# The four HGRN value tiles as one token-major group at the head of the layer

## The chip, the cores and the metric

The program runs on one core of one Trainium2 chip. The metric is the device time of one execution in microseconds. The engines are TensorE (PE; PEld is its weight load), VectorE (DVE), ScalarE (ACT), GpSimd (POOL) and SyncE (SP), which issues most of the DMAs.

## What is computed

Two layers over 640 tokens (128 of context, 512 latent; five token tiles of 128), model width 2048 (16 k-tiles), all in float32. Cut to what matters here, a layer is

```
h = x * (1 + scale) + shift                  # adaLN, from the conditioning vectors
z = h @ w_in_l                               # 2048 -> 6656 columns
aq, ak, av, ag, hq, hi, hff, hfb, hgate, ca, cb, cgate = split(z)
v = hi                                       # HGRN values, 4 heads of 128
hg_out = rms_norm(hgrn2(silu(hq), v, gates(hff)) + hgrn2 backward (gates(hfb)))
att = windowed attention with a sink;  cv = conv module
mix = concat(att * silu(ag), hg_out * silu(hgate), cv * silu(cgate))
x = LayerNorm(ALPHA * x + gate * (mix @ w_out_l))
```

Only `hi` (512 columns of `w_in`) and the order of the other tiles are concerned. A float32 product is made of three float32r matmuls: every operand is split into a high and a low part (`HH`, `HL` for the activations, two `wh` slots for a weight chunk), and high x high, high x low and low x high are accumulated.

## The kernel before

The activations lie as `HH`/`HL`: 128 model channels in the partitions, by token tile and k-tile. The projection is made in 52 tiles of 128 output columns (`NTILES`), feature-major: `mm` (L1162) takes a 128x128 weight block as the stationary operand and streams the 640 tokens past it, as 256 tokens (L1173) and 384 (L1175) into two PSUM banks. A tile is 16 k-tiles x 3 products x 2 matmuls. Two such PSUM tiles (`zt`) alternate; four single banks (`mb`) serve everything else.

The order of the tiles is: for each HGRN head j the tiles `hff`, `hfb`, `hi`, `hq`; then the four `hgate`; then attention's `ak`, `av`, `aq`; the conv tiles; the remaining gates. After each tile, a generator that evacuates it is put in the list `active`; behind `hq` also `hg_main` (L505), the HGRN computation of that head. The order of the instructions on each engine is written out by `pump` (L260): after every half of a weight chunk (eight times per tile) it advances up to three of the active generators by one step, and at a rate given by `RATE` the modulation of later stages, which `ada_dve` computes on VectorE (L362). If a PSUM tile or a scratch slot (`S`, nine of them) isn't free when the program is written, `pump_until` advances the generators until it is. `hg_main` takes 27 steps to the head's output; the heads hold a lock, one after the other, and there are two sets of HGRN buffers.

HGRN needs its values token-major (tokens in the partitions, as `lhsT` of L693 and right operand of L664), so `e_hi` (L482) copies the tile to scratch on ScalarE and `to_tokens` (L471) transposes it with five matmuls against the identity (L474, L478) and copies the result on ScalarE (L475, L479) into the head's buffer `v`.

Weights come in chunks of 128 x 512 float32 (256 KB), four to a tile. `w_load1` (L1117) loads one over SP into one of eight `raw` slots, `w_split` (L1129) splits it into two of 16 `wh` slots. The split has three forms: ScalarE copies the high part and VectorE subtracts (L286, L287); GpSimd does both (L284, L287); or ScalarE copies the high part and its negative (L290, L291) and a DMA from GpSimd's queue adds the weight from HBM onto it (L292, `split_add`). In the run of a layer the last form is used, one tile ahead (`ahead`, L1238).

**Start of layer 0.** `ada_pe` computes scale and shift on TensorE from 64 weight tiles of 512 KB (L317, ten `x` buffers), for eight pairs of k-tiles one after the other. `after0` (L1190) builds those two k-tiles of `HH`/`HL` and then, one pair late, issues the matmuls of the first three projection tiles on them (`start_mm`, L1184), into `zt[0]`, `zt[1]` and two single banks.

**Layer boundary.** The last output group has 256 columns; for each of the five token tiles TensorE makes 48 matmuls (L1482), VectorE adds to the residual `Y` and gathers statistics, `ln_norm` normalises the token tile (L1373 on VectorE, L1375 on ScalarE), and `ln_next` (L1377) transposes it in four quarters (L1384), each into a PSUM bank from a ring of four, which ScalarE empties with scale and shift (L1391) and VectorE or GpSimd splits into `HH`/`HL` (L284, L287). The transposes of token tile t stand behind the matmuls of t+1 on TensorE. Then the first two tiles of layer 1 are made in halves: the 256 first tokens of tile 0, the last token tile's transposes, the 256 first tokens of tile 1, then the 384 other tokens of both. The chunks of tile 0 are split on GpSimd during the last token tile's matmuls.

Of the kernel before, what the change touches and what calls it, by code (L numbers as in the profile page):

```python
# [34 lines left out]
NTILES = ([(n, j) for j in range(4) for n in ("hff", "hfb", "hi", "hq")]  # L35
          + [("hgate", j) for j in range(4)] + [("ak", 0), ("av", 0)] + [("aq", h) for h in range(4)]
# [5 lines left out]
LO0, LO1 = (0, 1, 2, 3), ()  # L42
# [3 lines left out]
WN = (0, 3, 4)  # L46
# [10 lines left out]
HOLD0 = 18  # L57
# [68 lines left out]
def trunk(ctx: ExitStack, tc: tile.TileContext, A: dict):  # L126
# [55 lines left out]
    HGT = (("kt", 2 * T), ("gg", 2 * T), ("q", T), ("v", T))  # L182
# [3 lines left out]
    def open_layer(l):  # L186
        outs[l] = region(f"o{l}", "left", [(f"h{j}", T) for j in range(4)])
        for j in range(4):
            mix[l, 8 + j] = outs[l][2][f"h{j}"]
        for st in range(2):  # L190
            hgr[l, st] = region(f"h{l}{st}", SIDE[st], HGT)

# [30 lines left out]

    def zput(z):
        if isinstance(z, tuple):
            M.put(*z)
        else:
            ZP.put(z)

# [69 lines left out]
    def ada_pe(jobs, raws, after):  # L299
# [3 lines left out]
        for (part, nch), kq in tiles:  # L303
            while nxt < len(tiles) and raws:
                (p2, n2), k2 = tiles[nxt]
                r = raws.popleft()
                sync.dma_start(out=r, in_=A["adaw0"][p2, n2, k2])
                fly.append(r)
                nxt += 1
                if nxt == W0:  # L310
                    for i in range(NS):
                        w_load1(0, i, 0)
# [123 lines left out]
    def hv(*st):  # L436
        t = hgr[st][2]
        return t["kt"], t["gg"], t["q"], t["v"]
# [4 lines left out]
    def e_hf(l, j, d, z):  # L443
# [9 lines left out]
        act.activation(kd, zsb(z), AF.Sigmoid, scale=-1.0)  # L453
# [17 lines left out]
    def to_tokens(vT, v):  # L471
        b0 = yield from M.get()
        for c in range(4):
            pe.transpose(b0[:, 128 * c:128 * c + 128], vT[:, 128 * c:128 * c + 128], ident)  # L474
        act.copy(v[:, 0:512], b0)  # L475
        M.put(b0)
        b1 = yield from M.get()
        pe.transpose(b1[:, 0:128], vT[:, 512:640], ident)  # L478
        act.copy(v[:, 512:640], b1[:, 0:128])  # L479
        M.put(b1)  # L480

    def e_hi(l, j, z):  # L482
        yield from wait(("hgset", l, j))
        v = hv(l, hgset[l, j])[3]
        s = yield from S.get()
        if isinstance(z, tuple):
            act.copy(s[:, 0:256], z[0][:, 256:512])
            act.copy(s[:, 256:640], z[1][:, 0:384])
        else:
            act.copy(s[:, 0:T], zsb(z))  # L490
        zput(z)
        yield
        yield
        yield from to_tokens(s[:, 0:T], v)
        S.put(s)
        flags.add(("hi", l, j))
# [8 lines left out]
    def hg_main(l, j):  # L505
        yield from wait(("hf", l, j, 0), ("hf", l, j, 1), ("hi", l, j), ("hq", l, j))
        lk = yield from lock["hg"].get()
        st = hgset[l, j]
        Kt, GG, q, v = hv(l, st)
# [597 lines left out]
    def evac(l, name, j, z):  # L1107
# [4 lines left out]
        return {"hi": e_hi, "hq": e_hq, "ak": e_ak, "av": e_av, "aq": e_aq, "cb": e_cb, "ca": e_ca}[name](l, j, z)  # L1112
# [4 lines left out]
    def w_load1(l, i, c):  # L1117
        pump_until(lambda: RAW.f)
        r = RAW.take()
        sync.dma_start(out=r, in_=A["win"][l, i, c])  # L1120
        wraw[l, i, c] = r

    def w_load(l, i):
        for c in range(4):
            w_load1(l, i, c)
# [3 lines left out]
    def w_split(l, i, c, lo_eng=None, hi_eng=None):  # L1129
        pump_until(lambda: len(WH.f) >= 2)  # L1130
        hi, lo = WH.take(), WH.take()
        r = wraw.pop((l, i, c))
        if lo_eng == "dma":
            split_add(hi, lo, r, A["win"][l, i, c])
        else:
            split(hi, lo, r, lo_eng, hi_eng)
        wsp[l, i, c] = (hi, lo)
# [24 lines left out]
    def mm(l, i, z, ks, halves):  # L1162
        za, zb = (z[0][:, 256:512], z[1][:, 0:384]) if isinstance(z, tuple) else (z[:, 256:512], z[:, 512:896])
        za = za.rearrange("p (a b) -> p a b", b=P)
        zb = zb.rearrange("p (a b) -> p a b", b=P)
        for k in ks:
            hi, lo = wsp[l, i, k // 4]
# [8 lines left out]


    NS = 3
    zs = [zt[0], zt[1], (mb[2], mb[3])]
    M.f = deque(mb[0:2])  # L1180
    ZP.f.clear()
    for k in range(6):
        load_x0(k)
    def start_mm(n):  # L1184
        for i in range(NS):
            mm(0, i, zs[i], (2 * n, 2 * n + 1), (0, 1))
            if n % 2:
                WH.put(*wsp.pop((0, i, n // 2)))

    def after0(part, n):  # L1190
# [4 lines left out]
        if n % 2 == 0:  # L1195
            for i in range(NS):
                w_split(0, i, n // 2)
        for c in range(1, 4):
            if n == WN[c - 1]:
                for i in range(NS):  # L1200
                    w_load1(0, i, c)
        if n == 7:
            w_load(0, NS)
            for c in range(4):
                w_split(0, NS, c)
            w_load(0, NS + 1)
# [11 lines left out]
    for l in range(DEPTH):  # L1218
# [16 lines left out]
        first = NS if l == 0 else 2  # L1235
        wnext = 4 * (first + 2)

        def ahead(i, c):  # L1238
            nonlocal wnext
            m = 4 * (i + 1) + c  # L1240
            if i + 1 < NN:
                w_split(l, i + 1, c, "dma")
            else:
                o_split(l, c)
            while wnext <= m + (WLH if 0 in hold else WLA):
                if wnext < 4 * NN:
                    w_load1(l, wnext // 4, wnext % 4)
                else:
                    o_load(l, wnext - 4 * NN)
                wnext += 1  # L1250

        for i in range(first):
            enqueue(i, zs[i] if l == 0 else zt[i])
        for i in range(first, NN):
            pump_until(lambda: ZP.f)
            z = ZP.f.popleft()
# [364 lines left out]
```

## Time and profile before

| | us |
|---|---|
| median of 3 runs (2240.1 to 2241.21) | 2241.13 |
| the profiled execution | 2247.12 |
| its span | 2245.3 |
| TensorE busy in it | 2177.4 |
| VectorE, ScalarE, GpSimd busy | 1457.9, 1144.7, 601.9 |

TensorE works almost without a break from 38 us on; the start is filled with the DMA of the modulation weights, and the layer boundary lies between 1126 and 1202 us. Durations of matmuls overlap in the trace, so the cost of one is read from start to start. Layer 0's HGRN stage lies between 128 and 420 us, layer 1's between 1202 and 1500.

### The profile page before, as it was taken

What the parts mean: (1) busy time and instruction counts of PE and PEld (TensorE: products, weight loads), DVE (VectorE), ACT (ScalarE), POOL (GpSimd) and SP (SyncE); (2) the same over time, 40 slices, a digit from 0 to 9 for tenths busy, and PEclk for the clock granted to TensorE, in tenths of its full rate; (3) what the DMA queues carried; (4) which work ended last, traced back from release to release, by engine and by line L of the source; (5) the groups of instructions that cost most, each with busy time, mean ns of one, the idle gap of its engine ahead of it and who ended that gap; (6) DMA issues with size and microseconds to landing.
All of it is one profiled execution on the core that took longest, in us unless ns stands there. A gap on an engine that the chain in (4) does not pass through costs nothing.

```text
span 2245.3 us, 42128 instructions
## 1 busy us (share of the span) xinstructions
PE 2177.4 (97%) x15854; PEld 2076.1 (92%) x15854; DVE 1457.9 (65%) x3799; ACT 1144.7 (51%) x2051; POOL 601.9 (27%) x690
## 2 busy tenths in 40 slices
PE   5899999999999999999989999999999999999997
PEld 2699999999999999988989999999999999998887
DVE  2478899557669999766673666543654779225457
ACT  1267877546565435511155787774555543462112
POOL 0033344332222343300032344433222123331003
PEclk9999999999999999999999999999999999999999
DMA  9978787897766888964426777778776576676333
GB/s 358 392 206 199 185 209 182 201 219 173 176 159 155 206 193 212 259 233 128 128 108 158 156 172 162 162 173 189 160 163 137 110 173 147 150 164 212 99 99 123
DMA packets 210557, 403.61 MB, mean 180 GB/s; under 512 B 24656, under 2 KB 30512, under 8 KB 209712
## 3 DMA queue, kind: packets, MB, share of 16 engines
q1 hardware_dynamic: 138992, 271.85, 38.4%
q0 software_dynamic: 61440, 116.96, 30.2%
q10 hardware_dynamic: 9920, 12.10, 1.7%
q8 instruction: 124, 2.03, 0.4%
q14 instruction: 81, 0.66, 0.1%
HBM read 383.46 MB, written 12.11 MB: 176 GB/s over the span
## 4 chain that ended last, share of the span: by engine, by line
PE 75%; DVE 9%; DMA 6%; issue 5%; ACT 3%; POOL 1%; ACTq 1%; SPq 0%; POOLq 0%; DVEq 0%
PE z L1175 29%; PE z L1173 19%; PE z L1431 9%; PE m L1431 8%; DVE junk L362 4%; DMA x<-adaw 2%; PE m L948 2%; PE m L1482 2%; PE m L862 1%; DMA s<-xT 1%; PE m L916 1%; DMA s<-s 1%; DMA wh<-win 1%; PE m L664 1%; ACT s L1391 1%
## 5 line engine op out<-in xcount | busy, mean ns | idle before, releaser
L1175 PE MATMUL z<-HH,wh 128*128 128x384 f32 x3296 | 1046.6, 339 | 0.0
L1173 PE MATMUL z<-HH,wh 128*128 128x256 f32 x3296 | 926.6, 283 | 1.9 <-DMA wh<-win 1.0
L292 POOL DMA_DIRECT2D wh<-win x388 | 345.2, 936 | 1095.3 <-ACT wh L291 1024.0
L1173 PEld LDWEIGHTS z<-HH,wh 128*128 128x128 f32 x3296 | 619.5, 189 | 5.8 <-DVE wh L287 1.6
L1175 PEld LDWEIGHTS z<-HH,wh 128*128 128x128 f32 x3296 | 620.6, 188 | 1.5
L1175 PE MATMUL z<-HL,wh 128*128 128x384 f32 x1648 | 558.2, 339 | 0.0
L362 DVE SCALAR_TENSOR_TENSOR junk<-raw,s 128x256 bf16<-128x256 f32 x1024 | 502.5, 491 | 53.2 <-DMA raw<-adawD 25.0
L1173 PE MATMUL z<-HL,wh 128*128 128x256 f32 x1648 | 461.6, 280 | 0.0
L1173 PEld LDWEIGHTS z<-HL,wh 128*128 128x128 f32 x1648 | 310.9, 189 | 0.0
L1175 PEld LDWEIGHTS z<-HL,wh 128*128 128x128 f32 x1648 | 310.4, 188 | 0.0
L291 ACT ACTIVATE wh<-wh 128x512 fp32r<-128x512 f32 x400 | 253.0, 633 | 78.5 <-PE z L1175 67.4
L290 ACT CAST wh<-raw 128x512 fp32r<-128x512 f32 x400 | 244.0, 610 | 72.0 <-issue 36.1
L286 ACT CAST wh<-raw 128x512 fp32r<-128x512 f32 x136 | 83.0, 621 | 305.0 <-PE m L1431 153.8
L1027 DVE SCALAR_TENSOR_TENSOR s<-s,sm,s 128x655 f32<-128x655 f32 x240 | 229.6, 957 | 6.3
L1431 PE MATMUL z<-wh,HH 128*128 128x512 f32 (+1 forms) x640 | 182.1, 368 | 0.0
L1431 PE MATMUL m<-wh,HH 128*128 128x512 f32 (+1 forms) x640 | 173.8, 357 | 0.0
L287 DVE TENSOR_TENSOR wh<-raw,wh 128x512 fp32r<-128x512 f32 x138 | 92.6, 687 | 119.5 <-ACT wh L286 119.5
L1431 PEld LDWEIGHTS z<-wh,HH 128*128 128x128 f32 x640 | 116.1, 189 | 20.1
L1431 PEld LDWEIGHTS m<-wh,HH 128*128 128x128 f32 x640 | 114.2, 189 | 17.6
L1431 PE MATMUL z<-wh,HL 128*128 128x512 f32 (+1 forms) x320 | 117.8, 368 | 0.0
L1431 PE MATMUL m<-wh,HL 128*128 128x512 f32 (+1 forms) x320 | 114.4, 358 | 0.0
L1096 ACT ACTIVATE s<-z 128x640 f32<-128x640 f32 x32 | 22.5, 703 | 152.5 <-PE z L1175 143.7
(561 smaller groups left out, 2718.6 us busy)
## 6 DMA issues: line engine op xcount, KB each, us to landing
raw<-win SPq DMA_DIRECT2D x416, 256.0 KB, 4.2
wh<-win POOLq DMA_DIRECT2D x388, 256.0 KB, 5.6
raw<-adawD SPq DMA_DIRECT2D x256, 256.0 KB, 4.2
x<-adaw SPq DMA_DIRECT2D x64, 512.0 KB, 8.3
raw<-wout SPq DMA_DIRECT2D x128, 256.0 KB, 2.7
s<-crow SPq DMA_DIRECT2D x32, 256.0 KB, 5.9
s<-xT ACTq DMA_DIRECT2D x16, 320.0 KB, 7.5
s<-s ACTq DMA_DIRECT2D x80, 64.0 KB, 3.9
```

Source lines behind the costliest of these rows:

```text
L286: act.copy(hi, src)
L287: (lo_eng or dve).tensor_tensor(lo, src, hi.bitcast(F32), op=ALU.subtract)
L290: act.copy(hi, r)
L291: act.activation(lo, hi.bitcast(F32), AF.Copy, scale=-1.0)
L292: pool.dma_start(out=lo, in_=w.bitcast(F32R), accum_op=ALU.add)
L362: dve.scalar_tensor_tensor(junk, r[:, 256 * n:256 * n + 256], 1.0, rows[0][:, 256 * c:256 * c + 256], op0=ALU.mult, op1=ALU.mult, accum_ou ...
L948: pe.matmul(o, lhsT=v_, rhs=p_, start=(y == 0 and n_ == 0), stop=(y == len(bl) - 1 and n_ == 2))
L1027: dve.scalar_tensor_tensor(acc, u[:, t:t + AW], sm[:, cw + t:cw + t + 1], acc, op0=ALU.mult, op1=ALU.add)
L1173: pe.matmul(za, lhsT=w_, rhs=h_[:, 0:2, k, :], start=st_, stop=sp_)
L1175: pe.matmul(zb, lhsT=w_, rhs=h_[:, 2:5, k, :], start=st_, stop=sp_)
L1431: pe.matmul(bs[tt][:, 0:w], lhsT=h_[:, tt, k, :], rhs=w_[:, o:o + w], start=(k == 0 and n_ == 0), stop=(k == KT - 1 and n_ == 2))
L1482: pe.matmul(b[:, 0:w], lhsT=h_[:, tt, k, :], rhs=w_[:, o:o + w], start=(k == 0 and n_ == 0), stop=(k == KT - 1 and n_ == 2))
```

## The change

`hi` is no longer among the tiles; 48 remain, in the order `hff`, `hfb`, `hq` for heads 0 and 1, `hgate` 0, head 2, `hgate` 1, head 3, `hgate` 2 and 3, and then as before. Ahead of them a layer computes the values of all four heads as one group, token-major: the 512 columns of `hi` are the moving operand, a 128x128 block of `HH`/`HL` the stationary one, and each token tile has a PSUM bank of its own (five banks: both `zt` and `mb[2]`), 240 matmuls of 512 columns in all. `e_hi`, `to_tokens` and the buffer `v` go; five copies (three on ScalarE, two on VectorE) bring the group into the tile `h` that also takes the heads' outputs. The weights of the group are a new array of 16 chunks, one per k-tile. The first single tile of a layer goes into two single banks.

In the start of layer 0 the group takes the place of the first three tiles, with two chunks loaded and split per step. At the boundary all eight `raw` slots are loaded ahead; the eight chunks are split during the last token tile's matmuls, even ones on GpSimd, odd ones with the adding DMA; k-tiles 0 and 1 of the group for token tiles 0 to 2 stand ahead of the transposes of token tile 3, k-tiles 2 to 7 ahead of those of token tile 4, then the rest. The ring of banks for the transposes has three banks. `HOLD0` and the bounds of `RATE` move with the four tiles that are gone.

```diff
-NTILES = ([(n, j) for j in range(4) for n in ("hff", "hfb", "hi", "hq")]
-          + [("hgate", j) for j in range(4)] + [("ak", 0), ("av", 0)] + [("aq", h) for h in range(4)]
+NTILES = ([(n, j) for j in (0, 1) for n in ("hff", "hfb", "hq")] + [("hgate", 0)]
+          + [(n, 2) for n in ("hff", "hfb", "hq")] + [("hgate", 1)]
+          + [(n, 3) for n in ("hff", "hfb", "hq")] + [("hgate", 2), ("hgate", 3)]
+          + [("ak", 0), ("av", 0)] + [("aq", h) for h in range(4)]
...
+    def evac_hi(l, G):
+        h = outs[l][2]["h"].rearrange("p (j t) -> p j t", j=4)
+        for c in (1, 4, 0, 3, 2):
+            o, i = h[:, :, 128 * c:128 * c + 128], G[c].rearrange("p (j t) -> p j t", j=4)
+            if c > 2:
+                dve.tensor_copy(o, i)
+            else:
+                act.copy(o, i)
+        ZP.f = deque(zt)
+        M.put(mb[2])
...
+    def mm_hi(l, G, k, tts):
+        hi, lo = wsp[l, k]
+        for tt in tts:
+            for n_, (h_, w_) in enumerate(((HH, hi), (HH, lo), (HL, hi))):
+                pe.matmul(G[tt], lhsT=h_[:, tt, k, :], rhs=w_, start=(k == 0 and n_ == 0),
+                          stop=(k == KT - 1 and n_ == 2))
...
     def start_mm(n):
-        for i in range(NS):
-            mm(0, i, zs[i], (2 * n, 2 * n + 1), (0, 1))
-            if n % 2:
-                WH.put(*wsp.pop((0, i, n // 2)))
+        for k in (2 * n, 2 * n + 1):
+            mm_hi(0, G, k, range(TT))
+            WH.put(*wsp.pop((0, k)))
...
-            w_load(l + 1, 0)
-            w_load(l + 1, 1)
-            obank = [mb[2], zh[1], zh[3], zh[1], zh[3]]
-            banks = deque(mb[3:] + mb[:3])
+            w_load(l + 1, *range(8))
+            G = [zl[0], zl[1], mb[2], zf[0], zf[1]]
+            obank = [mb[2], zl[0], zf[0], zl[0], zf[0]]
+            banks = deque(mb[3:] + mb[:2])
...
-                    if not last and k < 8:
-                        w_split(l + 1, 0, k // 2, pool if k // 2 in LO0 else None, pool)
+                    if not last:
+                        if k % 4 == 1:
+                            w_split(l + 1, k // 2, pool, pool)
+                        else:
+                            w_split(l + 1, k // 2, "dma")
...
+                if tt == TT - 1:
+                    for k in range(2):
+                        mm_hi(l + 1, G, k, range(3))
                 g = ln_next(tt - 1) if tt > 0 else iter(())
...
-            mm(l + 1, 0, zt[0], range(KT), (0,))
-            g = ln_next(TT - 1)
-            for c in range(4):
-                w_split(l + 1, 1, c, pool if c in LO1 else None, pool)
-                next(g, None)
-            next(g, None)
+            for k in range(2, 8):
+                mm_hi(l + 1, G, k, range(3))
+            for _ in ln_next(TT - 1):
+                pass
             yp.release()
             open_layer(l + 1)
-            mm(l + 1, 1, zt[1], range(KT), (0,))
...
+            for k in range(8):
+                mm_hi(l + 1, G, k, (3,))
+            nq = 8
+            for k in range(KT):
+                mm_hi(l + 1, G, k, (4,) if k < 8 else range(TT))
+                WH.put(*wsp.pop((l + 1, k)))
...
```

## Rows read from the trace of the kernel before

**Rows 1.** The page, part 1: busy us, share of the span, instructions.

```profile
PE 2177.4 (97%) x15854; PEld 2076.1 (92%) x15854; DVE 1457.9 (65%) x3799; ACT 1144.7 (51%) x2051; POOL 601.9 (27%) x690
```

**Rows 2.** TensorE's waits over the whole span: total us, times, longest us.

```profile
PE m L317 <- DMA x<-adaw: 22.8, 15, 6.6
...
PE m L540 <- DVE s L534: 4.8, 5, 1.4
PE m L540 <- DVE s L607: 4.6, 5, 1.3
```

**Rows 3.** Windows: length, busy PE, PEld, DVE, ACT, POOL; clock, DMA share, GB/s.

```profile
38.08:117.06 78.98, 64.38 (x624) 47.04 (x625) 33.59 (x81) 13.41 (x21) 0.00 (x0) 0.94 1.01 387
...
1126.30:1201.90 75.60, 68.24 (x515) 65.83 (x514) 49.56 (x96) 43.78 (x101) 20.09 (x18) 1.00 0.34 119
...
245.70:315.30 69.60, 67.59 (x633) 66.69 (x633) 60.40 (x164) 55.26 (x88) 27.34 (x31) 1.00 0.81 195
```

**Rows 4.** Timeline, start of layer 0: last modulation transposes; ScalarE takes the fourth tile.

```profile
117.06 0.44 PE L327 MATMUL m<-ident,s 128*128 128x128 f32 x2 [0.55 <-DVE s L323]
...
142.73 0.70 ACT L500 ACTIVATE h00q<-z 128x640 f32<-128x640 f32 x1 [3.33 <-PE z L1175]
```

**Rows 5.** Timeline of TensorE (start, us): a k-tile apart, three matmuls apart, transposes.

```profile
429.81 0.28 PE L1173 MATMUL z<-HH,wh 128*128 128x256 f32 x1
...
430.69 0.28 PE L1173 MATMUL z<-HH,wh 128*128 128x256 f32 x1
...
1059.77 0.39 PE L1431 MATMUL z<-wh,HL 128*128 128x512 f32 x1
...
1060.45 0.39 PE L1431 MATMUL z<-wh,HL 128*128 128x512 f32 x1
...
133.18 0.60 PE L474 MATMUL m<-ident,s 128*128 128x128 f32 x4
133.61 0.27 PE L478 MATMUL m<-ident,s 128*128 128x128 f32 x1
```

**Rows 6.** Chain that ended last, layer boundary: start us, us, what.

```profile
1126.35 5.76 PE m L1482 x48
...
1185.27 14.74 PE z L1175 x85
```

**Rows 7.** Timeline at the layer boundary: start, us, engine; idle before in brackets.

```profile
1155.40 0.66 PE L1384 MATMUL m<-ident,y0y 128*128 128x128 f32 x4 [0.72 <-ACT s L1391]
...
1163.58 1.62 PE L1384 MATMUL m<-ident,y0y 128*128 128x128 f32 x12 [1.77 <-ACT s L1391]
...
1163.01 5.67 ACT L1391 ACTIVATE s<-m,shf,scl 128x128 f32<-128x128 f32 x16
...
1158.07 1.63 POOL L287 TENSOR_TENSOR wh<-raw,wh 128x512 fp32r<-128x512 f32 x1
...
1160.53 1.61 POOL L287 TENSOR_TENSOR wh<-raw,wh 128x512 fp32r<-128x512 f32 x1
...
1156.98 0.53 DVE L284 CAST HH<-s 128x512 fp32r<-128x512 f32 x1
...
1158.45 1.52 DVE L284 CAST HH<-s 128x512 fp32r<-128x512 f32 x1
```

**Rows 8.** The adding DMA by its line: issue ns, landing; the page's group before it.

```profile
L292 POOL DMA_DIRECT2D wh<-win x388: 836/862/1938, 132.2 to 1990.4; - x194
...
DMA to landing us min/median/max: 3.7/5.6/10.8
...
L291 ACT ACTIVATE wh<-wh 128x512 fp32r<-128x512 f32 x400 | 253.0, 633 | 78.5 <-PE z L1175 67.4
```

**Rows 9.** Attention of layer 0: a wait of TensorE, and the window behind it.

```profile
525.05 0.58 PE L862 MATMUL m<-a00k,a00qa 128*128 128x384 f32 x1 [2.21 <-DVE ats L877]
...
525.00:540.00 15.00, 14.95 (x96) 14.95 (x97) 9.83 (x38) 9.56 (x23) 3.60 (x5) 0.89 0.82 207
```

**Rows 10.** Timeline: ScalarE copies the output of HGRN head 0.

```profile
198.19 0.58 ACT L699 COPY o0h<-m 128x512 f32<-128x512 f32 x1 [4.05 <-PE m L695]
```

More of the change, by code (lines that the diff above doesn't have):

```diff
@@ L186, in open_layer @@
     def open_layer(l):
-        outs[l] = region(f"o{l}", "left", [(f"h{j}", T) for j in range(4)])
+        outs[l] = region(f"o{l}", "left", [("h", 4 * T)])
         for j in range(4):
-            mix[l, 8 + j] = outs[l][2][f"h{j}"]
+            mix[l, 8 + j] = outs[l][2]["h"][:, T * j:T * j + T]
         for st in range(2):
@@ L222, in trunk, with __init__, zparts @@
     S.put(crs)
+    class Z:
+        def __init__(self, a, b):
+            self.a, self.b, self.banks = a[:, 256:512], b[:, 0:384], (a, b)
     def zput(z):
-        if isinstance(z, tuple):
-            M.put(*z)
+        if isinstance(z, Z):
+            M.put(*z.banks)
         else:
             ZP.put(z)
+    def zparts(z):
+        if isinstance(z, Z):
+            return (slice(0, 256), z.a), (slice(256, T), z.b)
+        return ((slice(0, T), z[:, 256:896]),)
     def load_consts():
@@ L310, in ada_pe @@
                 if nxt == W0:
[L311 to L312 removed]
+                    w_load(0, *range(4))
             if kq == 0:
@@ L505, in hg_main @@
     def hg_main(l, j):
-        yield from wait(("hf", l, j, 0), ("hf", l, j, 1), ("hi", l, j), ("hq", l, j))
+        yield from wait(("hf", l, j, 0), ("hf", l, j, 1), ("hq", l, j))
         lk = yield from lock["hg"].get()
         st = hgset[l, j]
-        Kt, GG, q, v = hv(l, st)
+        Kt, GG, q, v = hv(l, st, j)
         ae = aE[j % 2]
@@ L1111, in evac, with w_src, w_load, w_split @@
             return e_gate(l, j + {"ag": 0, "hgate": 8, "cgate": 12}[name], z)
-        return {"hi": e_hi, "hq": e_hq, "ak": e_ak, "av": e_av, "aq": e_aq, "cb": e_cb, "ca": e_ca}[name](l, j, z)
+        return {"hq": e_hq, "ak": e_ak, "av": e_av, "aq": e_aq, "cb": e_cb, "ca": e_ca}[name](l, j, z)
     wraw = {}
[L1117 to L1125, printed above, removed]
+    def w_src(l, q):
+        return A["whi"][l, q] if q < NG else A["win"][l, q - NG]
+    def w_load(l, *qs):
+        for q in qs:
+            pump_until(lambda: RAW.f)
+            r = RAW.take()
+            sync.dma_start(out=r, in_=w_src(l, q))
+            wraw[l, q] = r
     wsp = {}
-    def w_split(l, i, c, lo_eng=None, hi_eng=None):
+    def w_split(l, q, lo_eng=None, hi_eng=None):
         pump_until(lambda: len(WH.f) >= 2)
         hi, lo = WH.take(), WH.take()
-        r = wraw.pop((l, i, c))
+        r = wraw.pop((l, q))
         if lo_eng == "dma":
-            split_add(hi, lo, r, A["win"][l, i, c])
+            split_add(hi, lo, r, w_src(l, q))
         else:
             split(hi, lo, r, lo_eng, hi_eng)
-        wsp[l, i, c] = (hi, lo)
+        wsp[l, q] = (hi, lo)
         RAW.put(r)
@@ L1194, in after0 @@
         build_h0(2 * n + 1)
[L1195 to L1201, printed above, removed]
+        w_split(0, 2 * n)
+        w_split(0, 2 * n + 1)
+        w_load(0, 2 * n + 4, 2 * n + 5)
         if n == 7:
[L1203 to L1206, printed above, removed]
+            for q in range(NG, NG + 4):
+                w_split(0, q)
+            w_load(0, *range(NG + 4, NG + 8))
         if n > 0:
@@ L1263, in trunk @@
                 mm(l, i, z, (4 * c + 2, 4 * c + 3), (0, 1))
-                WH.put(*wsp.pop((l, i, c)))
-                ahead(i, c)
+                WH.put(*wsp.pop((l, NG + 4 * i + c)))
+                ahead(NG + 4 * i + c)
                 pump(3, rate)
             enqueue(i, z)
-        nload = wnext - 4 * NN
+        nload = wnext - NQ
         nsplit = 4
```

110 lines of the change are left out of this document (44 added, 66 removed).

## The prediction

> **What bounds the kernel now.** I read the head of the page first: TensorE is busy 2177 of 2245 us [rows 1]. So an edit pays in two ways only: it takes TensorE work away, or it fills one of the 68 us in which TensorE stands idle. The table of TensorE's waits says where these are [rows 2]: 23 us for the modulation weights at the start (L317), and a few us in HGRN's small matmuls (L540); at the layer boundary it waits ahead of the transposes (L1384) [rows 7]. The windows show the same from the other side [rows 3]: from the first value matmul to the last modulation job (38.08 to 117.06) 14.6 us are idle while the DMA engines are full; from the last output group of layer 0 to the end of layer 1's first two tiles (1126.3 to 1201.9) 7.4 us; and a whole HGRN head period is 97% TensorE with VectorE at 87%. The timelines gave the pace of the matmuls [rows 5], and the order on ScalarE and GpSimd at the boundary [rows 7].
>
> **Pace of the two forms.** A k-tile of one projection tile is three pairs of 256 and 384 columns; it takes 430.69 - 429.81 = 0.88 us, 0.293 a pair [rows 5]. Three matmuls of 512 columns take 1060.45 - 1059.77 = 0.68 us, 0.227 each [rows 5]. Per column the pair costs 0.458 ns and the 512 form 0.443 ns. Solving the two gives about 13 ns a matmul beside 0.417 ns a column.
>
> **Start of layer 0.** Before, three tiles are accumulated between the modulation jobs, 2 x 3 x 3 pairs = 5.28 us a step; after, the group of four heads, 2 x 3 x 5 matmuls of 512 = 6.80 us. Six steps lie between 38 and 117 us, two behind it. TensorE's added 6 x 1.52 = 9.1 us fit into its 14.6 us idle there [rows 3]. What is paid is DMA: 16 chunks instead of 12 are queued ahead of the last modulation weights, 1.05 MB at 387 GB/s [rows 3] = 2.7 us (the chunks issued after them don't count). The last job's transposes end at 117.5 [rows 4]; after at 120.2, plus two steps of 6.8: the group is ready at 133.8. Before, four tiles are done when ScalarE takes the fourth at 142.7 [rows 4], one head's transposes included. That is 8.9 us. Were none of the 9.1 us hidden, the group would end at 117.5 + 9.1 + 13.6 = 140.2 and the gain be 2.5; were the DMA cost hidden too, 11.6. The waits come in clumps, so not all fits: I take **8.0**.
>
> **Transposes.** Each head's value tile needs five transposes; four and then the next start 0.43 us apart [rows 5], so 0.54 us a head. Eight heads lose them, one of which is counted above: 7 x 0.54 = **3.8**. The copies out of them on ScalarE, and the first copy, go as well; five copies of 512 columns come per layer. ScalarE and VectorE have idle time beside TensorE there, so I take nothing for them.
>
> **Matmuls of layer 1's values.** 192 pairs x 0.293 = 56.3 us become 240 x 0.227 = 54.4: **1.9**. Of the fixed cost of a matmul the Trainium skill ("TensorE: Matmul & The Clock Gate", section "Wait — 56ns, not 53.3ns?") says about 2.5 ns; by it this term would be 144 x 2.5 ns = 0.4 us. The row shows five times that for this kernel's float32r operands, and the row decides.
>
> **Layer boundary.** Work in the window: 240 matmuls at 5.76/48, 80 transposes at 0.108, 96 first halves at 0.12, 96 second halves at 14.74/85 [rows 6]: 28.8 + 8.6 + 11.5 + 16.6 = 65.5 of 75.6, so 10.1 us are lost now (what the 7.4 leaves is pipeline fill). After, three things change.
> (a) The transposes of the normalised rows turn over three PSUM banks, not four: the fourth quarter of a token tile must wait until ScalarE has emptied the first of the same tile. ScalarE does 16 such copies in 5.67 us [rows 7], 1.42 a quarter; from token tile 1 on it stands behind two quarters of the tile before. I estimate 0.9 + 1.4 + 1.4 = 3.7 us more for token tiles 0 to 2, beside some 1.0 lost there now (one wait of 0.72 [rows 7] and a smaller one).
> (b) Every second weight chunk of the new group takes its low part by a DMA that adds: two ScalarE passes, 2 x 0.63 us, an issue on GpSimd and 5.6 us to landing [rows 8]. These passes are put on ScalarE behind the norm of token tile 3 and the 8 copies after it: 1163.01 + 2.83 [rows 7], + 2.3 for (a) = 1168.1. Chunk 1's low part lands at 1168.1 + 1.3 + 5.6 = 1175.0. TensorE ends the last output group at 1163.58 - 1.77 = 1161.8 now [rows 7], so at 1165.5; it does k-tile 0 in nine matmuls (2.04 us), one of k-tile 1, and wants that low part at 1167.7. Queued behind it are the next transposes, and for these wait ScalarE, VectorE and layer 1's activations. So 7.3 us; 5.4 to 12.5 with the shortest and longest landing, none if ScalarE comes to it early.
> (c) A wait of 2.2 us in attention stands in a stretch of 15 us whose granted clock is 0.89 [rows 9]: 3.3 us of it at 1.2 GHz, not 2.4, so about 1.7 us more behind such a wait, or nothing.
> The longer cover (six k-tiles, 12.2 us, ahead of the last transposes) leaves about 1.0 of waits there. Sum after: 1.0 + 3.7 + 7.3 + 1.0 + 1.7 = 14.7 against 10.1: **-4.6** (bounds +4.4 and -9.8).
>
> **HGRN.** Head 0 starts a whole group later, and heads follow each other after three tiles, or four where a gate tile stands between. A head needs 27 steps to its result; eight are given per tile, so 3.4 tiles. Head 0 took 142.7 to 198.2 for them [rows 10]. After its last tile, head 3 has two gate tiles, one key and one value tile (56 us and 10.7 of its own TensorE work, which is 67.6 - 56.3 - 0.5 [rows 3]) before the query tile that needs it: covered by 11 us. A gate tile holds a slot of scratch until its head is done, head 3's for two tiles, and the key tile gets its three slots only when head 3 gives up its own, about half a tile before a PSUM tile is wanted: tight, but no forced wait. VectorE's load falls on a shorter head: 60.4 us in the 32 steps between two heads [rows 3] are between 51 (if all of it shrinks with the steps) and 60.4 (if nothing does) in 3.4 x 14.1 + 10.7 = 58. I take nothing, -4 to +3. The modulation of layer 1 on VectorE loses eight steps of its schedule in layer 0, as there is one tile less that pumps it, and ends later in the output projection, where VectorE isn't full: nothing, or up to -2 if the rest falls between the last two output groups.
>
> **Sum.** 8.0 + 3.8 + 1.9 - 4.6 = 9.1 us. The profiled execution took 2247.1 (span 2245.3 and 1.8 around it), so 2238.0 for one like it; the median of the runs is 6.0 below it: **2232**. Its own range is 2227 to 2237.
>
> **Rivals.**
> A. The boundary doesn't stall: ScalarE reaches chunk 1 in time. For it speaks that ScalarE is busy only 43.8 of these 75.6 us [rows 3]; against it the order of its queue. 9.1 + 4.6 + 4.4 = 18.1: 2223. Chance 0.18.
> B. The start hides nothing: TensorE's steps become the bound of the start, for which speaks that the last job waited for VectorE alone, for no DMA [rows 4]. 9.1 - 5.5 = 3.6: 2238. Chance 0.12.
> C. Slower: GpSimd paces the group at the boundary. A pair of chunks costs it a split (2.46 us from one to the next [rows 7]) and an issue; TensorE needs one pair per 2 x 2.04 = 4.1 us, and this decides: above 4.1 us TensorE waits at every pair. While GpSimd splits, a VectorE copy took 1.52 instead of 0.53 us [rows 7], so the two hold each other up. If each pair also waits for its landing, 2.46 + 0.86 + 5.6 = 8.9 [rows 7, 8], three further pairs lose 4.8 each: 9.1 - 14.4 = -5.3: 2246.4. Against it: an issue doesn't wait for its landing. The Trainium skill ("SBUF — State Buffer", section "SBUF: two separate sides") has the rule for this: an exclusive lock on ports that VectorE and GpSimd share, which also keeps GpSimd from writing a DMA's descriptors. The stretched copies bear out the lock; no row shows starved descriptors. Chance 0.08.
> D. HGRN at the higher density loses to VectorE: the waits of L540 double (9.4 us now [rows 2]) once VectorE needs more than the 58 us of a head. 9.1 - 8 = 1.1: 2240. Chance 0.12.
> The forecast keeps 0.50.
>
> **How the numbers follow.** About 0.2% (4.5 us) is what a measurement tells from no change, so faster means below 2236.6 and slower above 2245.6. Faster: 0.47 of the forecast's 0.50, all of A, 0.05 of B, 0.03 of D: 0.73. Slower: most of C and a tail of D's: 0.07. Same: 0.20. The range 2222 to 2241 takes in the forecast, B, D and A but for its lower part; C is left out.
>
> **What would show it.** The value matmuls of layer 0 end near 134 us. No transpose of value tiles is left, and the 512-column value matmuls start 0.227 us apart. At the boundary one wait of 5 us or more stands ahead of a (low part) matmul of k-tile 1, released by a DMA; without it, A. Waits at several odd k-tiles: C. Waits for modulation weights all but gone and a group that ends at 138 or later: B. Waits at L540's lines above 15 us: D. I'd be wrong altogether if TensorE waited for head 3 ahead of attention, which I hold to be covered.

## The result and the profile after

| | median us (runs) | profiled execution: span | TensorE clock, mean |
|---|---|---|---|
| before | 2240.88 (4) | 2245.3 | 0.994 |
| after | 2265.27 (4; 2265.13 to 2269.28) | 2263.5 | 0.987 |

The changed kernel is **slower**: ratio 1.0114, 95% interval 1.0096 to 1.0131, 24.4 us where 9.1 less were forecast, and outside the range given. The two profiled executions differ by 18.2 us only, since that of before lay 6.2 above its median (with its 1.8 us around the span). One run of e3 below took 2882.0 us at a granted clock of 0.70 and is left out of e3's time.

In the changed kernel `mm` is L1170 and L1172, the group's matmul L1178, the adding DMA L305 (its ScalarE passes L303, L304), HGRN's matmuls of 128, 64 and 32 columns L565, L570 and L537, the modulation on VectorE L374. The kernels of the experiments have them up to two lines away. In HGRN, a level of a head is made by two subtractions on GpSimd (L518, L521), two exponentials on ScalarE (L524, L525), two multiplications on VectorE (L530, L531) and then TensorE. A head ends with a norm: squares, sums on TensorE (L439), a logarithm (L713) and an exponential (L716) on ScalarE, a product on VectorE (L718).

By stage, in the two profiled executions (borders: four tiles or the group and no tile done; ScalarE's copy of the first key tile; the last output group's first matmul):

| stage | before | after | difference |
|---|---|---|---|
| start of layer 0 | 142.7 | 130.5 | -12.2 |
| HGRN of layer 0 | 291.7 | 309.8 | **+18.1** |
| attention to output, layer 0 | 691.9 | 694.5 | +2.6 |
| layer boundary | 103.6 | 104.0 | +0.4 |
| HGRN of layer 1 | 285.4 | 298.0 | **+12.6** |
| rest | 730.0 | 726.7 | -3.3 |

The start gave more than forecast and the boundary cost less; 30.7 us were lost in the two stages for which the prediction took nothing. TensorE's waits in the changed kernel, over the whole span (total us, times, longest; they answer to [rows 2]):

```profile
PE m L329 <- DMA x<-adaw: 17.4, 12, 6.3
PE m L570 <- DVE s L531: 16.2, 4, 8.0
...
PE m L537 <- DVE s L531: 9.8, 8, 1.7
PE z L1178 <- DMA wh<-whi: 4.7, 1, 4.7
...
PE m L1383 <- ACT s L1390: 3.0, 4, 0.8
PE m L537 <- DVE s L604: 2.0, 2, 1.3
```

The row of L570 is new: two long waits, one in each layer. The windows (columns as in [rows 3]; the first 117 us, the HGRN stages of both layers) of the kernel before:

```profile
0.00:117.00 117.00, 82.11 (x758) 52.05 (x758) 42.38 (x107) 19.84 (x32) 3.00 (x12) 0.94 0.99 376
142.70:434.40 291.70, 284.02 (x2626) 280.37 (x2626) 242.76 (x666) 221.54 (x352) 116.53 (x126) 1.00 0.81 194
1229.90:1515.30 285.40, 283.77 (x2630) 280.83 (x2629) 163.99 (x410) 220.81 (x352) 115.59 (x127) 1.00 0.74 166
```

and of the changed one, with two short stretches behind waits of layer 0:

```profile
0.00:117.00 117.00, 87.76 (x726) 51.51 (x727) 43.65 (x110) 20.89 (x34) 3.00 (x12) 0.99 0.99 385
130.50:440.30 309.80, 292.25 (x2628) 287.78 (x2627) 244.13 (x662) 219.54 (x346) 118.02 (x127) 0.97 0.76 184
1238.80:1536.80 298.00, 286.80 (x2627) 283.46 (x2626) 177.74 (x420) 218.89 (x346) 117.07 (x127) 0.98 0.70 158
...
247.00:254.00 7.00, 7.00 (x44) 6.88 (x45) 6.90 (x7) 3.86 (x7) 5.99 (x5) 0.55 0.51 78
...
404.00:415.00 11.00, 10.76 (x92) 10.70 (x93) 10.71 (x28) 5.83 (x9) 3.00 (x3) 0.71 0.58 145
```

VectorE's busy time in layer 0's stage is the same (243 and 244 us), so it is no busier there; in layer 1 it rose from 164 to 178. TensorE's idle time (length less busy PE) went from 7.7 to 17.6 us in layer 0 and from 1.6 to 11.2 in layer 1, so 9.9 and 9.6 us of the two losses are waits. The granted clock has fallen as well: 1.00 to 0.97 in layer 0, some 9 of 309.8 us (part of it lies beside waits), and 0.98 in layer 1; that is of the size of the rest, 8.2 and 3.0. Behind the long wait it is 0.55, so nearly all at 1.2 GHz and not 2.4; behind the short waits of head 3 it is 0.71.

The long wait of layer 0, at the passage from head 0 to head 1 (the "seam"; no gate tile stands there). Timeline: start us, us, engine; idle before in brackets:

```profile
235.95 0.89 POOL L305 DMA_DIRECT2D wh<-win  x1 [4.30 <-ACT wh L304]
236.55 1.57 POOL L518 TENSOR_TENSOR s<-h01gg 128x640 f32<-128x640 f32 x1
237.77 1.60 POOL L521 TENSOR_TENSOR s<-h01gg 128x640 f32<-128x640 f32 x1
...
238.16 0.74 ACT L524 ACTIVATE s<-s 128x640 f32<-128x640 f32 x1 [2.51 <-POOL s L518]
239.41 0.74 ACT L525 ACTIVATE s<-s 128x640 f32<-128x640 f32 x1 [0.52 <-POOL s L521]
240.16 1.28 ACT L713 ACT_TABLE_LOAD   x1
241.46 0.94 ACT L713 ACTIVATE s<-m,eps 128x384 f32<-128x384 f32 x2
242.42 1.28 ACT L716 ACT_TABLE_LOAD   x1
243.71 0.74 ACT L716 ACTIVATE s<-s 128x640 f32<-128x640 f32 x1
...
244.48 0.88 DVE L718 SCALAR_TENSOR_TENSOR o0h<-o0h,sm,s 128x640 f32<-128x640 f32 x1 [8.12 <-ACT s L716]
...
246.02 0.82 DVE L531 SCALAR_TENSOR_TENSOR s<-s,h01q 128x640 f32<-128x640 f32 x1
...
246.98 1.33 PE L570 MATMUL m<-s,s 128*64 128x64 f32 x20 [7.53 <-DVE s L531]
...
247.21 6.15 DVE L374 SCALAR_TENSOR_TENSOR junk<-raw,s 128x256 bf16<-128x256 f32 x1
...
247.64 1.58 POOL L518 TENSOR_TENSOR s<-h01gg 128x640 f32<-128x640 f32 x1
248.86 1.65 POOL L521 TENSOR_TENSOR s<-h01gg 128x640 f32<-128x640 f32 x1
250.17 1.55 POOL L518 TENSOR_TENSOR s<-h01gg 128x640 f32<-128x640 f32 x1
251.38 1.69 POOL L521 TENSOR_TENSOR s<-h01gg 128x640 f32<-128x640 f32 x1
```

Read it from TensorE backward. L570 waits for L531, whose own input was there at 240.15; it stands behind L718, head 0's norm product, for which VectorE is idle 8.12 us. L718 waits for an exponential that stands on ScalarE behind two table loads, a logarithm and head 1's exponentials, and these waited for GpSimd, 2.51 and 0.52 us. An idle VectorE makes its load (rival D) an unlikely cause of this wait. The last five rows show a second thing: one L374, usually 0.42 us, took 6.15 us beside four of GpSimd's subtractions.

### The profile page after: what moved, and what is told of

Read it like the earlier page. It is cut to its first block, busy times and chain, and to the rows that moved or that the text cites. A ratio compares the mean times of both kernels' runs of the same rounds, so it can differ in the third digit from the quotient of the medians.

```text
span 2263.5 us, 41414 instructions
## 1 busy us (share of the span) xinstructions
PE 2179.4 (96%) x15526; PEld 2058.0 (91%) x15526; DVE 1469.7 (65%) x3809; ACT 1129.8 (50%) x2028; POOL 593.1 (26%) x680
## 4 chain that ended last, share of the span: by engine, by line
PE 71%; DVE 10%; issue 7%; DMA 5%; ACT 3%; POOL 2%; ACTq 1%; POOLq 0%; SPq 0%; DVEq 0%
PE z L1172 24%; PE z L1170 16%; PE z L1430 9%; PE m L1430 8%; DVE junk L374 4%; PE z L1178 3%; DVE s L1024 2%; PE m L945 2%; DMA x<-adaw 2%; PE m L1481 2%; PE m L859 1%; DMA wh<-win 1%; DMA s<-xT 1%; PE m L913 1%; POOL wh L305 1%
## 5 line engine op out<-in xcount | busy, mean ns | idle before, releaser
L1172 PE MATMUL z<-HH,wh 128*128 128x384 f32 x3008 | 962.2, 340 | 0.0
L1170 PE MATMUL z<-HH,wh 128*128 128x256 f32 x3008 | 852.0, 283 | 1.1 <-DMA wh<-win 1.0
L305 POOL DMA_DIRECT2D wh<-win x380 | 337.4, 933 | 1136.5 <-ACT wh L304 1086.1
L1170 PEld LDWEIGHTS z<-HH,wh 128*128 128x128 f32 x3008 | 569.4, 189 | 4.8 <-DMA wh<-win 1.9
L1172 PEld LDWEIGHTS z<-HH,wh 128*128 128x128 f32 x3008 | 569.1, 189 | 1.4
L374 DVE SCALAR_TENSOR_TENSOR junk<-raw,s 128x256 bf16<-128x256 f32 x1024 | 508.7, 497 | 46.1 <-DMA raw<-adawD 20.4
L1172 PE MATMUL z<-HL,wh 128*128 128x384 f32 x1504 | 510.9, 340 | 0.0
L1170 PE MATMUL z<-HL,wh 128*128 128x256 f32 x1504 | 422.1, 281 | 0.0
L303 ACT CAST wh<-raw 128x512 fp32r<-128x512 f32 x396 | 241.4, 610 | 101.9 <-issue 41.1
L304 ACT ACTIVATE wh<-wh 128x512 fp32r<-128x512 f32 x396 | 250.5, 632 | 76.0 <-PE z L1172 65.1
L1170 PEld LDWEIGHTS z<-HL,wh 128*128 128x128 f32 x1504 | 284.7, 189 | 0.0
L1172 PEld LDWEIGHTS z<-HL,wh 128*128 128x128 f32 x1504 | 284.5, 189 | 0.0
L1178 PE MATMUL z<-wh,HH 128*128 128x512 f32 x256 | 80.8, 396 | 4.7 <-DMA wh<-whi 4.7
```

Source lines behind the costliest of these rows:

```text
L303: act.copy(hi, r)
L304: act.activation(lo, hi.bitcast(F32), AF.Copy, scale=-1.0)
L305: pool.dma_start(out=lo, in_=w.bitcast(F32R), accum_op=ALU.add)
L374: dve.scalar_tensor_tensor(junk, r[:, 256 * n:256 * n + 256], 1.0, rows[0][:, 256 * c:256 * c + 256], op0=ALU.mult, op1=ALU.mult, accum_ou ...
L1170: pe.matmul(za, lhsT=w_, rhs=h_[:, 0:2, k, :], start=st_, stop=sp_)
L1172: pe.matmul(zb, lhsT=w_, rhs=h_[:, 2:5, k, :], start=st_, stop=sp_)
```

## The experiments

Theory S: the order in the queues at the seam costs the two long waits and the lower clock behind them. Theory V: rival D, VectorE has too much to do at three tiles a head. R and Q are scratch or a late head 3; G, formed after e5 and e6, is GpSimd's subtractions. "Ratio" is against the kernel before, with its 95% interval.

**e1_lock: the next head starts after the norm.**

```diff
-        lock["hg"].put(lk)
         for _ in range(RY):
             yield
...
         S.put(sq)
         flags.add(("mix", l, 8 + j))
+        lock["hg"].put(lk)
```

> Edit: in the changed kernel a head gives the lock that admits the next head up after its norm, not before it; nothing else moves. Theory S (the seam: where no gate tile stands between head 0 and head 1, head 0's norm product stands on VectorE ahead of head 1's first multiplications and itself waits for an exponential on ScalarE that is queued behind head 1's): the two waits of 7.53 and 7.98 us ahead of the 64-column HGRN products go, the 16.2 us of that row fall below 4, and with the stretch of lower granted clock behind each the time falls by 15 to 25 us, to 2240 to 2250. Theory V (rival D of the prediction: VectorE has too much to do per head): a later start of a head gives VectorE no more time, so that row stays above 10 us and the time at 2260 to 2270. Theory R (the denser heads run out of scratch slots or PSUM): a head that starts later holds its slots longer, 2265 to 2285.

Measured 2264.46 us, ratio 1.0103 (1.0088 to 1.0118). TensorE's waits:

```profile
PE m L537 <- DVE s L531: 15.7, 9, 3.7
...
PE m L570 <- DVE s L531: 5.4, 4, 2.0
PE m L565 <- DVE s L531: 3.3, 2, 1.7
```

A miss: the long waits of L570 go, as S says, but are spread over L565 and L537 of the same head. The seam is not one misplaced instruction.

**e2_late: the norm product four steps later.**

```diff
-        yield
+        for _ in range(5):
+            yield
```

> Edit: in the changed kernel the norm product of a head (VectorE, L718) is issued four steps later; lock, tiles and all else stay. Theory S with VectorE's queue as the place of the block: head 1's first multiplication no longer stands behind that product, its own inputs were there at 240.14 us against a wait that ended at 246.98, so the waits of 7.53 and 7.98 us fall to 2.5 or less, and the time by 10 to 22 us, to 2243 to 2255. If the block is rather on ScalarE (head 0's logarithm, its table loads and exponential ahead of head 1's exponentials), the wait only shrinks to some 4 to 6 us and the time to 2255 to 2262. Theory V (VectorE's load): no change, 2262 to 2268.

Measured 2258.51, ratio 1.0082 (1.0067 to 1.0097): 6.8 us better than the changed kernel. TensorE's waits:

```profile
PE m L537 <- DVE s L531: 10.1, 10, 1.7
PE z L1171 <- DMA wh<-win: 5.7, 6, 2.6
...
PE m L570 <- DVE s L531: 3.6, 2, 2.0
```

The longest wait of L570 falls from 8.0 to 2.0, so the norm product in VectorE's queue was its last link. But the time lies in the range that was expected if the block were on ScalarE, under half of the gain that VectorE's queue promised. Weights, whose two ScalarE passes stand in the same queue as the logarithm, come late in its place.

**e3_gates: all gate tiles behind the heads, as before.**

```diff
-NTILES = ([(n, j) for j in (0, 1) for n in ("hff", "hfb", "hq")] + [("hgate", 0)]
...
+NTILES = ([(n, j) for j in range(4) for n in ("hff", "hfb", "hq")]
+          + [("hgate", j) for j in range(4)]
```

> Edit: the changed kernel with the order of its single tiles undone: all four gate tiles behind the four heads, as in the kernel before; the group of value tiles stays. So three seams of a layer have no gate tile between heads, where the changed kernel has one. Theory S: each such seam brings a wait of 7 to 8 us of the 64-column products on VectorE's multiplication and some 5 us of lower clock; the row goes from 16.2 us in all to 35 to 50, and the time rises by 25 to 50 us, to 2290 to 2315. Theory V (VectorE's load): heads are denser, so waits grow as well but spread over many steps, not one long wait per seam. Theory R (the gate tiles between the heads are what costs, by the scratch slots that they hold): the time falls to 2240 to 2255.

Measured 2279.62, 95% interval of the ratio 1.0158 to 1.0198. Its waits:

```profile
PE m L569 <- DVE s L530: 31.0, 4, 8.0
...
PE m L564 <- ACT wh L303: 4.7, 2, 2.4
```

Two long waits a layer, where S expected three; the third seam waits 2.4 us only. The direction is S's, the size (14 us, not 25 to 50) is not. R falls.

**e4_rate: half the modulation on VectorE in layer 0's HGRN stage; e8_before_rate: the same in the kernel before.**

```diff
-RATE = ((1.0, 0.85, 0.5, 1.2), (0.5, 0.5, 0.0, 0.8))
+RATE = ((0.5, 0.85, 0.5, 1.2), (0.5, 0.5, 0.0, 0.8))
```

> Edit: in the changed kernel the pace at which layer 1's modulation is pumped through VectorE while layer 0's HGRN tiles run is halved (1.0 to 0.5 of a job a step); it is done later instead, in the stages behind. Theory V (rival D, VectorE's load at the higher density): the wait of 7.53 us at 247 us in layer 0 shrinks to under 4, HGRN of layer 0 gets shorter by 5 to 10 us. Theory S: VectorE stands idle ahead of that wait anyway, so it stays at 6 to 8 us. The whole time says little here (the modulation may end too late for layer 1), the stage alone is read.

> Edit: the kernel before, with layer 1's modulation pumped at half the pace through VectorE in layer 0's HGRN stage, as in e4_rate: a control for what VectorE's load costs each of the two kernels. In the changed kernel that shortened layer 0's HGRN stage (end of the value tiles to the first key tile) by 10.9 us. If the kernel before gains as much, the load isn't what the change brought; if it gains 3 to 6 us (its 7.7 us of waits there), the other 5 to 8 us are the price of denser heads (theory V beside theory S). The whole time is not read (the modulation ends too late).

In e4 the waits of layer 0's HGRN stage are

```profile
PE m L570 <- DVE s L531: 7.9, 2, 7.5
PE m L537 <- DVE s L604: 2.0, 1, 2.0
PE m L537 <- DVE s L531: 0.4, 1, 0.4
```

So the long wait stays with half the load (S), while the short ones of L537, 7.9 us in the changed kernel there, all but go (V). From ScalarE's pass over head 0's `hq` (L497, before L500) to that over attention's first query tile (L809, before L812), layer 0 got 11.1 us shorter in e4 (293.9 to 282.8) and 6.5 in e8 (320.4 to 313.9). That is just above the 3 to 6 us that e8 was to give if density has a price of its own. The difference, 4.6 us, is what VectorE's load costs the changed kernel beyond what it cost the kernel before, from one execution of each. The whole times, 2317.2 and 2290.4, say nothing here: the modulation ends too late for the boundary.

**e5_all: a gate tile behind every head. e6_move: the seam without a gate tile moved to heads 2/3.**

The first line is e5's, the others are e6's.

```diff
+NTILES = ([x for j in range(4) for x in [(n, j) for n in ("hff", "hfb", "hq", "hgate")]]
...
+NTILES = ([(n, j) for j in (0, 1) for n in ("hff", "hfb", "hq", "hgate")]
+          + [(n, j) for j in (2, 3) for n in ("hff", "hfb", "hq")] + [("hgate", 2), ("hgate", 3)]
```

> Edit: in the changed kernel every head gets its gate tile right behind it (head 0, gate 0, head 1, gate 1 and so on), so no seam is left without one and every head has four tiles of time. Theory S (seam): no wait of 7 to 8 us is left in either layer, the row of the 64-column products falls from 16.2 us to under 4. Theory V (VectorE's load per head at three tiles a head): the waits of L537 in layer 0, 7.9 us, fall as well. By both the time is 2240 to 2252. Rival Q (head 3 now has one gate tile, one key and one value tile behind it, not two gate tiles): the query tile of attention waits for head 3 or for scratch, a new wait of 5 to 12 us per layer ahead of attention, and the time is 2255 to 2270.

> Edit: in the changed kernel the gate tiles stand behind heads 0, 1 and (two of them) 3, so the one seam without a gate tile moves from heads 0/1 to heads 2/3. Theory S: the wait of 7 to 8 us moves with it, to about 310 to 330 us of layer 0 and 100 us or more later in layer 1 than now, and none is left at heads 0/1; the time stays within 2258 to 2270. Were it the start of a layer (the first head after the value tiles, the first use of a table) that costs, no such wait is left or it stays at heads 0/1: 2245 to 2255, or 2265 with the wait at 247.

Measured 2271.81, ratio 1.0143 (1.0126 to 1.0160), and 2262.91, ratio 1.0100 (1.0085 to 1.0115). Both are misses for S as it stood, though e6's time lies in S's range, and e5 is one for V: every head has four tiles again, as before the change, and TensorE waits 26.0 us in layer 0's HGRN stage, where the changed kernel waits 17.6. In e6 no long wait moved to heads 2/3; in both, layer 0 now waits 2.7 and then up to 6.0 us at the seams *with* a gate tile. In layer 1, at half the modulation rate, no wait over 2.8 us is left in either. The wait of e5 in its timeline:

```profile
255.27 5.90 DVE L529 SCALAR_TENSOR_TENSOR s<-s,h01q 128x640 f32<-128x640 f32 x1
...
255.06 1.58 POOL L516 TENSOR_TENSOR s<-h01gg 128x640 f32<-128x640 f32 x1
...
258.94 1.53 POOL L519 TENSOR_TENSOR s<-h01gg 128x640 f32<-128x640 f32 x1
...
261.22 1.01 PE L568 MATMUL m<-s,s 128*64 128x64 f32 x14 [5.98 <-DVE s L529]
```

The multiplication itself takes 5.90 us, not 0.82, from the start of four subtractions on GpSimd to their end. In the changed kernel that stall hit an L374 that nobody waited for; here it hits what TensorE waits for. Hence theory G. (e5 also waits 7.9 us at the boundary for the late modulation, which is in its time.)

**e7_bound: chunk 1 of layer 1's values split on GpSimd.**

```diff
-                        if k % 4 == 1:
+                        if k % 4 == 1 or k == 3:
```

> Edit: in the changed kernel chunk 1 of layer 1's value weights is split whole on GpSimd, as chunk 0 is, and not by two ScalarE passes and an adding DMA. If the one wait of 4.7 us at the layer boundary (the matmul of k-tile 1 on its low part) is due to that chunk's place behind ScalarE's 8 copies, it goes, with no other in its place: layer 1 starts 4 to 6 us earlier, 2259 to 2262. Rival: GpSimd is then behind by one split (2.5 us) for chunks 2 and 4, and TensorE waits there for 2 to 5 us: 2262 to 2268.

Measured 2259.48, ratio 1.0083 (1.0068 to 1.0098): 5.8 us better than the changed kernel. The wait of L1178 is gone and none stands in its place at the boundary; a hit.

**e9_late_bound: e2 and e7 together.**

> Edit: the changed kernel with the edits of e2_late and e7_bound together. If the seam and the boundary are two causes in two places, their gains add: 2265.3 - 6.8 - 5.8 = 2252.7, so 2250 to 2256. If what the one gives back is taken by the other (a layer that starts earlier meets later weights), 2257 to 2260.

Measured 2256.10, ratio 1.0068 (1.0053 to 1.0083). At the edge of what adding says; 2.4 us better than e2 alone. Inconclusive on its own.

**e10_lev: the levels' subtractions on VectorE; e12_before_lev: the same in the kernel before.**

```diff
-            pool.tensor_tensor(cap(el[:, 0:T], 0, [[h, 2], [2 * h, nb], [1, h]]),
+            dve.tensor_tensor(cap(el[:, 0:T], 0, [[h, 2], [2 * h, nb], [1, h]]),
...
-            pool.tensor_tensor(cap(er[:, 0:T], h, [[-h, 2], [2 * h, nb], [1, h]]),
+            dve.tensor_tensor(cap(er[:, 0:T], h, [[-h, 2], [2 * h, nb], [1, h]]),
```

> Edit: in the changed kernel the subtractions ahead of the exponentials of a level (L518, L521; eight a head, 1.5 to 1.7 us each on GpSimd) run on VectorE. Theory G: VectorE is held while GpSimd subtracts (one L374 of 0.42 us took 6.15 us at 247.21, beside four of them), and head 0's logarithm on ScalarE at 240.16 stands behind exponentials that wait for GpSimd; so these subtractions are what makes the seam long. Then no VectorE instruction of over 2 us is left in that stage beside those that stand behind others' GpSimd work, the wait of 7.53 us falls to 2 to 4, and the time to 2248 to 2258. Rival: VectorE has no room for eight more instructions of some 0.8 us a head in layer 0 (244 of 310 us busy there), so layer 0's waits on it grow by more than is saved: 2262 to 2275.

> Edit: the kernel before with the subtractions of e10_lev on VectorE. A control: its heads have four tiles of time and no seam wait, so little is to be had: theory G with the seam says 2236 to 2242 (at most the 7.7 us of short waits in layer 0 fall by half). If it gains as much as the changed kernel does, moved subtractions say nothing about the change.

Measured 2240.52, ratio 0.9999 (0.9990 to 1.0009), so 24.8 us better than the changed kernel; and 2229.82, ratio 0.9952 (0.9937 to 0.9966), 10.8 better than before: more than expected in both, and the control beats the kernel before by itself. Groups between 130 and 445 us (count, busy us, mean ns) of the changed kernel:

```profile
L521 POOL TENSOR_TENSOR s<-h01gg 128x640 f32<-128x640 f32 x8 | 13.2, 1650 | 0.0
...
L374 DVE SCALAR_TENSOR_TENSOR junk<-raw,s 128x256 bf16<-128x256 f32 x262 | 149.8, 572 | 7.9 <-DMA s<-crow 0.8 <-DMA raw<-adawD 0.5
```

of the kernel before:

```profile
L362 DVE SCALAR_TENSOR_TENSOR junk<-raw,s 128x256 bf16<-128x256 f32 x281 | 165.9, 590 | 12.5 <-DMA s<-crow 3.4 <-DMA raw<-adawD 1.8
```

of e10:

```profile
L518 DVE TENSOR_TENSOR s<-h01gg 128x640 f32<-128x640 f32 x8 | 6.6, 819 | 0.0
...
L374 DVE SCALAR_TENSOR_TENSOR junk<-raw,s 128x256 bf16<-128x256 f32 x282 | 120.7, 428 | 10.2 <-DMA raw<-adawD 2.9 <-DMA s<-crow 0.5
```

and TensorE's one wait in e10's stage:

```profile
PE m L570 <- DVE s L531: 4.8, 1, 4.8
```

VectorE does a subtraction in 0.82 us, GpSimd in 1.5 to 1.65; and the modulation's mean falls from 572 to 428 ns, so by this estimate VectorE had stood still for 262 x 0.144 = 38 us there. Eight more instructions a head therefore cost it nothing. The standstill is not new: in the kernel before the same instruction had a mean of 590 ns, and one of them took 6.16 us at 223.70, beside four subtractions. What is new is which work stands behind it. All waits of L537 go, and the long one shrinks by 2.7 to 4.8: head 1's exponentials no longer wait 2.51 and 0.52 us for GpSimd. The edit changes several things at once (the standstill, the length of a subtraction, its place ahead of the exponentials), and no run takes them apart.

**e11, e13, e14, e15: what is left.** e11 is e10 with the edits of e2 and e7; e13 is e10 with e7; e14 is e13 with the norm product two steps later; e15 is e13 with the lock of e1.

> Edit: the changed kernel with the edits of e2_late, e7_bound and e10_lev together. If the three causes are separate, 2265.3 less their three gains, 2236 to 2246, which would be level with the kernel before or below it; if the late norm product and the moved subtractions cure the same wait, 2245 to 2254.

> Edit: the changed kernel with the moved subtractions (e10_lev) and the boundary's edit (e7_bound). If the boundary is a cause of its own, it is worth here what it was worth alone (5.8 us): 2233 to 2237; the seam's two waits of 4.8 us stay. If the gain of 24.8 us already held a part of it: 2238 to 2241.

> Edit: e13 with the norm product issued two steps later (e11 has it four steps later). If what is left of the seam is the norm product ahead of head 1's multiplications in VectorE's queue, the waits of 4.8 us fall below 1 us in both layers and the time is 3 to 7 us below e13, 2227 to 2234. If the block is ScalarE (the logarithm with two table loads ahead of the weight passes), TensorE waits for weights in its place, as it does for 7.9 us in all in e11, and the time is within 2 us of e13.

> Edit: e13 with the lock of a head given up after its norm, as in e1_lock. In e1 that moved the waits (to 3.7 us ahead of the 32-column products) and gained 0.8 us. If GpSimd's subtractions were what made them late there, no wait of over 1.5 us is left in HGRN here and the time is 4 to 9 us below e13, 2226 to 2233. If a head needs more than its three tiles whatever runs first, waits of 2 to 4 us stand later in head 1, and the time is within 2 us of e13.

| | us | ratio to before |
|---|---|---|
| e11 | 2231.90 | 0.9962 (0.9951 to 0.9974) |
| e13 | 2235.72 | 0.9977 (0.9967 to 0.9986) |
| e14 | 2231.26 | 0.9953 (0.9938 to 0.9968) |
| e15 | 2230.82 | 0.9949 (0.9934 to 0.9963) |

The boundary is worth 4.8 us here (e10 to e13), near its 5.8 alone. What was left of the seam is worth 4.5 to 4.9. e13, e14 and e15 lie in their first ranges; e11 is below its 2236 to 2246, but 4.0 above what the gains of e2, e7 and e10 would add up to (2227.9), so these overlap. The waits of e14:

```profile
PE z L1172 <- DMA wh<-win: 7.4, 7, 1.7
...
PE m L570 <- DVE s L531: 0.2, 1, 0.2
```

The 7.4 us for weights are the sign that was expected if ScalarE were the block, so it has a part in it. In e15 the lock that had only moved the waits in e1 now works:

```profile
PE z L1170 <- DMA wh<-win: 3.6, 2, 1.9
PE m L570 <- DVE s L531: 1.8, 2, 0.9
PE m L565 <- DVE s L531: 1.5, 2, 1.2
```

e11, e13, e14 and e15 beat both kernels. e12, the old order with the subtractions moved, is as fast as any of them.

## Why the prediction was wrong

**The account.** With the subtractions on VectorE, changed and old kernel lie 2240.52 - 2229.82 = 10.7 us apart instead of 24.4. So 13.7 us of the loss hang on the subtractions standing on GpSimd in the changed order; 4.8 on the boundary's chunk 1 (e13), 4.9 on the rest of the seam (e15); 1.0 is left between e15 and e12. Each part is a difference of medians whose runs spread by 2 to 11 us, so it is good to some 2 us, and the 1.0 can't be told from nothing. How the 13.7 divide between VectorE's standstill and the later exponentials is not shown.

**HGRN, the step that failed: "I take nothing, -4 to +3".** It was +18.1 and +12.6 us. The step compared sums: 27 steps against 3.4 tiles, and VectorE's 51 to 60.4 us against a head's 58 [rows 3]. Both were beside the point. Of VectorE's 60.4 busy us 8.8 were the excess of two modulation instructions (3.52 and 6.16 us instead of 0.42) that stood still beside GpSimd, so they were no load; and what mattered was which instruction such a stall, or the norm of the head before, would stand ahead of in an in-order queue. The stretched copy at the boundary (1.52 instead of 0.53 us, [rows 7]) had shown the mechanism, but the prediction used it for that place only. The waits of L540 [rows 2] were small in the kernel before although VectorE stood still as long in layer 0, since there the modulation took it. Four tiles a head are not enough for that: e5 has them and waits up to 6.0 us.

**Rival D** named the place (these waits, from 9.4 us to 28.0 with L570; L537 alone has 11.8, under the 15 that was to be D's sign) and missed the price: 8 us and no clock. Its mechanism holds for 4.6 us in layer 0 (e4 against e8) and not for the long waits, which stood beside an idle VectorE and came in layer 1 too, at half the modulation.

**Start of layer 0.** Forecast 8.0. The group's last matmul starts at 130.1, two steps of 6.8 us behind the last transposes at 116.4, as worked out. The profiled pair shows 12.2, of which some 3 are the one execution of before: in e12, with the same start, ScalarE takes the fourth tile at

```profile
139.72 0.71 ACT L500 ACTIVATE h00q<-z 128x640 f32<-128x640 f32 x1 [3.33 <-PE z L1175]
```

so about 9. The 2.7 us of DMA were not paid: in the first 117 us 385 GB/s were moved instead of 376, 1.05 MB more, which is the four extra chunks. Rival B is refuted.

**Boundary: forecast -4.6.** (b) was right in place and cause: one wait at a low part of k-tile 1, released by the adding DMA, of 4.71 us where 7.3 were forecast (5.4 to 12.5), since it landed 4.3 us after its issue and not 5.6, and since ScalarE came to the chunk 1.2 us before TensorE wanted it (1173.0 and 1174.2) and not 0.4 after; e7 shows it by itself. (c) The lower clock behind it is in e7's 5.8. (a) failed: three banks cost nothing, the transposes wait 3.0 us against 6.4 before (4.5 for ScalarE's emptying, 1.9 for its normalisation):

```profile
PE m L1384 <- ACT s L1391: 4.5, 6, 1.8
...
PE m L1384 <- ACT y0y L1375: 1.9, 1, 1.9
```

Rivals A and C are refuted; no odd chunk but the first waits.

**Matmuls and transposes.** The group of layer 1 starts a matmul every 0.227 us in e15, where no clock is lost there, so the group's part of the 1.9 us was right, and with it the choice of the row's 13 ns a matmul over the Trainium skill's 2.5 ns ("TensorE: Matmul & The Clock Gate", section "Wait — 56ns, not 53.3ns?"). No value transpose is left, but the 3.8 us can't be seen as time.

**What stays open.** e15 has all three causes mended and yet isn't faster than e12, where start, transposes and matmuls should give some 14 us. By stage its start is 8.7 us ahead of e12; to attention's first query tile layer 0 gives back 2.4, layer 1 5.6, the stretch between 0.6. Windows show most of that: TensorE is idle for 2.1 us of e15's stretch in layer 0 and for 3.3 in layer 1 (1.9 of them one wait for weights), for none in e12's, and the clock is 0.99 there against 1.00, some 1.7 us in each. So the order with three tiles a head still costs short waits. Where the transposes' 3.8 us went wasn't traced to a cause.

## What to carry over

Before heads, or any chains, are packed closer, write down the queue of each engine at the passage from one chain to the next: the tail of the one (a norm with table loads) stands ahead of the head of the other, and busy shares don't show it. Look for single instructions that take many times their usual duration; such "busy" time is a wait. Here it stood in the trace of before, and the change decided on whom it fell. A late consumer is cured where its chain starts: moving the subtractions brought 24.8 us (10.8 in the kernel before too), moving the blocking product 6.8.

## What the hardware showed

A VectorE instruction with two inputs stood still while GpSimd ran four subtractions one after the other, 6.15 and 5.90 us where 0.42 and 0.82 are usual; it did not end between them. The Trainium skill ("SBUF — State Buffer", section "SBUF: two separate sides") has an exclusive lock on a shared port pair, held for a whole instruction, between a VectorE operation with two SBUF inputs and a GpSimd operation that reads SBUF. The traces agree with the lock; that it was kept through four GpSimd instructions goes beyond the sentence. A wait also cost more than its own length: behind one of 7.53 us TensorE was granted 0.55 over the next 7 us, by estimate some 3 us of its work.
